# A hybrid attention, convolution and ConvFFN block: up tiles of one side of two groups, sums in three batches, another opening

## The chip, the cores and the metric

The kernel runs on one core of a Trainium2 chip. The time is the device time of one execution in microseconds (us). A profiled execution gives the trace; its rows name the engines PE (matmul), PEld (PE's weight loads), DVE, ACT, POOL and SP. In this kernel SP issues nearly all transfers and POOL a few.

## The reference

One sequence of 256 tokens, width 2048, all float32. A conditioning vector c gives six vectors of 2048 (shift, scale and gate for each half of the block), and each half is a gated residual:

```python
mod = jax.nn.silu(c) @ w_ada[l] + b_ada[l]                # 2048 x 12288
sh1, sc1, g1, sh2, sc2, g2 = jnp.split(mod, 6, axis=-1)
h = modulate(rms_norm(x, norm1_g[l]), sh1, sc1)           # h * (1 + scale) + shift
proj = h @ w_in[l]                                        # 2048 x 6144
q, k, v, gb, gc, xt = jnp.split(proj, ...)                # 8 heads of 128 | 1024 conv channels
attn = moba_attention(q, k, v)                            # 256 tokens: one block, plain causal
conv = gb * causal_dwconv(gc * xt, conv_w[l], conv_b[l])
mixed = concat([rms_norm(attn, ...), rms_norm(conv, ...)])
x = x + g1 * (mixed @ w_out[l])                           # 2048 x 2048
h2 = modulate(rms_norm(x, norm2_g[l]), sh2, sc2)
u = causal_dwconv(h2 @ w_ffn_up[l], ffn_conv_w[l], ffn_conv_b[l])   # 2048 x 11264, 3 taps
u_gate, u_up = jnp.split(u, 2, axis=-1)
x = x + g2 * ((jax.nn.silu(u_gate) * u_up) @ w_ffn_down[l])         # 5632 x 2048
```

## The kernel before

Every float32 factor is split into a rounded part `hi` and a rest `lo`, and a product is made of three: hi·hi and hi·lo of the activations with `hi` of the weights, and hi of the activations with `lo` of the weights. A weight tile is 1 MB (128 x 4 x 512): SP loads it into one of seven `raw` buffers, ACT rounds it to `hi` (`split_hi`, L329), DVE subtracts to `lo` (`split_lo`, recorded at L166, the line of the helper through which most of DVE's work goes), and PE multiplies. There are three `hi` and three `lo` buffers. The work on one weight tile is a slot, and the slots follow one another on PE in a fixed order.

Opening. SP loads x, then four tiles of `w_ada` (L363) for the first 256 channels of the scale SC1 and the shift SH1, then weights of the projection. PE multiplies the four tiles with silu(c) (`ada`, L396) into partial sums on 128 rows; ACT copies them (`adae`), PE transposes the copy (`adac`, L453), DVE reduces it (`adaz`), and ACT adds it to the normed, scaled input `hf`, which gives the first `h`. Then the first projection product can run (L583). The other modulation tiles are spread over later slots by the table `ada`; each is consumed by PE or by DVE (L387, L389).

Projections. 48 tiles of `w_in` in the order of `turns` (L514 to L517), with attention and convolution between, to about 324 us; then `w_out`, to about 424 us.

Up. A group is 256 channels of each side (gate and up). Its slot k takes four of the 16 row blocks of `w_up`, 256 columns of the gate side and 256 of the up side, in two transfers of 512 KB (`up_slots`). The sixteen 512-wide products are L1057, the sixteen 256-wide ones L1060; they add up in four PSUM banks `z`. Groups 0 to 5 are done in two halves of the rows ('a' and 'b'; L1042 for the first four in 'a'). Groups 6 to 21 ('x') run from 570 us on. `up_sum` adds the halves of a bank on ACT and DVE (`ub`), `up_conv` and `up_conv_b` make the three-tap convolution (`uy`): a first tap on ACT, each further one on ACT (`tap`) with a sum on DVE, or as two STTs on DVE (scalar times tensor plus tensor). `up_silu` and `up_gate` make the product.

Down. The product with `w_down` of groups 0 to 15 is done by Strassen's scheme: seven products in place of eight. A group's `w_down` tile is used in two half slots, 'A' (three products' worth) and 'B' (four, from sums of blocks that DVE makes at L301, L304, L307), for each half `cp` of the columns (L994 to L998). Half slots stand between up slots; `places` in `plan` lists for every group behind which of its slots 0 to 3 they stand. At the end of a batch the bank sums `u` are copied (`pu`, ACT) and POOL adds them to DRAM (`down_sums`). `join_load` reads these back and `join_sum` joins them on DVE (`ju`). The last six groups go through twelve ordinary down slots (keys `('D', f)`), and `evac_down` writes the output. In these, `gate_down` multiplies with G2, whose modulation tiles are spread over the up slots.

What a slot's steps on ACT, DVE, SP and POOL are queued behind is set by tables: a step is hung to a slot (`at`), and the classes `cls` order the steps within a slot; `x_first` and `hi_late` set where `lo` and `hi` stand among them.

Of the kernel before, what the change touches and what calls it, by code (L numbers as in the profile page):

```python
# [59 lines left out]
       'taps': [1, 1, 2, 6],  # L60
# [10 lines left out]
       'slag': [[1, 2], [-1, 2]],  # L71
# [5 lines left out]
       'up': [[0, 2, 2, 4], [0, 0, 0, 0]],  # L77
       'gate': [3, 4, 7, 11],
# [6 lines left out]
               'conv_q': 0,  # L85
# [36 lines left out]
               'join_sum': 2},  # L122
       'up0': [[1, 1, 2, 4], [0, 1, 3, 3], [0, 2, 1, 2], [1, 1, 3, 5], [4, 4, 5, 8], [5, 5, 6, 9]],
# [16 lines left out]
       'part_lead': [4, 3, 2],  # L140
# [7 lines left out]
def tile_block(  # L148
# [77 lines left out]
    V.tensor_copy(identb, ident)  # L226

# [118 lines left out]
    class Ada:  # L346


        def __init__(self, part, c0, n, pe):
            self.part, self.c0, self.n, self.pe = part, c0, n, pe  # L350
            self.rows = 2048 // n
            self.tiles = NK // self.rows
            self.nch = n // P
            self.acc = None
            self.two = []
            self.used = 0

        def want(self, r):
            a = self.part * D + self.c0 * P
            k0 = r * self.rows  # L360

            def issue(t):
                nc.sync.dma_start(self.view(t), w_ada[0, k0 * P:(k0 + self.rows) * P, a:a + self.n]  # L363
                                  .rearrange("(k p) f -> p k f", p=P))
            return issue

# [172 lines left out]
    def pair_load(k, f):  # L539
        def issue(t):  # L540

            n = 1 if not slots_begun else 2
            slots_begun.append(f)
            for j in range(0, 2, n):
                nc.sync.dma_start(t.rearrange("p (k h) f -> p k (h f)", k=2)[:, j:j + n],
                                  w_in[0, (k + j) * P:(k + j + n) * P, COL[f] * 512:COL[f] * 512 + 1024]
                                  .rearrange("(k p) f -> p k f", p=P))
# [274 lines left out]
    def up_sum(grp, one):  # L822

        new = grp not in ub
        if one:
            if new:
                ub[grp] = [t2k(f"ub{grp}") for _ in range(2)]
            for ft in range(4):
                p, d = zp[grp][ft][:, :256], ub[grp][ft // 2][:, (ft % 2) * 256:(ft % 2) * 256 + 256]
# [4 lines left out]
            del zp[grp]  # L834
            return
        c = [t2k(f"ub{grp}") for _ in range(2)]
        for ft in range(4):
            act(c[ft // 2][:, (ft % 2) * 256:(ft % 2) * 256 + 256], zp[grp][ft][:, 256:], AF.Copy)  # L838
# [814 lines left out]
```

## Time and profile before

| | us |
|---|---|
| median of three runs | 1146.89 (1146.16 to 1148.3) |
| the profiled execution's own time | 1144.87 |
| its span, first to last instruction | 1143.1 |
| PE busy | 1128.9 (99%) |
| DVE busy | 1064.0 (93%) |
| ACT busy | 730.6 (64%) |
| moved by DMA | 363.66 MB, mean 318 GB/s |

A row of the timeline gives start, duration, engine, line, instruction, names and shapes, and in brackets the idle time ahead and who ended it. Runs of like instructions stand in one row with their number. The DMA share is the mean busy share of the core's 16 DMA engines.

### The profile page before, as it was taken

The page shows a single profiled execution, that of the slowest core. Times are in us where ns is not written, and L with a number is a line of the kernel's source. Part 1 is how long each engine was busy: PE and PEld are TensorE (multiplying, and loading weights), DVE is VectorE, ACT ScalarE, POOL GpSimd, SP SyncE. Part 2 cuts the span into 40 slices and gives each one's busy share as a digit, 9 for nine tenths or more (in the row PEclk, how much of TensorE's full clock was granted, in tenths as well). Part 3 has the DMA queues.
Part 4 walks back from the last instruction along what each step waited for, and adds up shares of the span by engine and source line. Part 5 has one row for each costly group of instructions (what it writes and reads, how often), then busy time and mean ns, then how long its engine had stood idle before and what let it go on. Part 6 is the DMA issues. An engine that isn't in the chain of part 4 may idle for free.

```text
span 1143.1 us, 16244 instructions
## 1 busy us (share of the span) xinstructions
PE 1128.9 (99%) x6035; PEld 953.8 (83%) x6035; DVE 1064.0 (93%) x1163; ACT 730.6 (64%) x1090; POOL 61.3 (5%) x90
## 2 busy tenths in 40 slices
PE   6999999999999999999999999999999999999998
PEld 4777778888888889988888888888888888888887
DVE  4789989989999998889999999899999999999798
ACT  4644455576786555566687676777677768866731
POOL 1000000000000000000000000101011101111000
PEclk9999999999999999999999999999999999999999
DMA  9999998998898899987679887999899988999951
GB/s 362 407 413 399 412 370 300 415 381 306 331 395 315 288 317 356 330 278 243 215 244 370 308 292 245 315 361 297 312 275 339 318 315 265 350 318 298 366 224 74
DMA packets 198687, 363.66 MB, mean 318 GB/s; under 512 B 9408, under 2 KB 108180, under 8 KB 194000
## 3 DMA queue, kind: packets, MB, share of 16 engines
q1 hardware_dynamic: 189152, 343.44, 82.8%
q0 software_dynamic: 8160, 17.04, 6.8%
q10 hardware_dynamic: 1296, 2.16, 0.5%
q8 instruction: 47, 0.77, 0.2%
q14 instruction: 32, 0.26, 0.1%
HBM read 343.70 MB, written 18.89 MB: 317 GB/s over the span
## 4 chain that ended last, share of the span: by engine, by line
PE 93%; DVE 3%; DMA 2%; SPq 1%; ACT 1%; issue 0%; DVEq 0%; ACTq 0%
PE z L1057 25%; PE z L1060 13%; PE u L996 4%; PE u L998 4%; PE u L994 4%; PE z L1042 4%; DMA raw<-in_w_in_dram 2%; DVE lo L166 2%; PE mk L516 1%; PE mk L517 1%; PE mk L514 1%; PE mx L516 1%; PE mc L516 1%; PE mq L517 1%; PE mg L516 1%; PE mx L517 1%
## 5 line engine op out<-in xcount | busy, mean ns | idle before, releaser
L329 ACT ACTIVATE hi<-raw 128x2048 fp32r<-128x2048 f32 (+1 forms) x227 | 417.8, 1857 | 260.5 <-DMA raw<-in_w_in_dram 73.2
L166 DVE TENSOR_TENSOR lo<-raw,hi 128x2048 fp32r<-128x2048 f32 (+2 forms) x229 | 501.7, 2200 | 23.0 <-ACT hi L329 17.7
L1057 PE MATMUL z<-h,hi 128*128 128x512 f32 x1280 | 303.3, 390 | 0.2 <-DVE ub L166 0.2
L1057 PEld LDWEIGHTS z<-h,hi 128*128 128x128 f32 x1280 | 237.8, 188 | 49.5 <-ACT hi L329 0.8
L389 DVE SCALAR_TENSOR_TENSOR ada<-raw,csil,ada 128x512 f32<-128x512 f32 (+3 forms) x167 | 195.7, 1175 | 5.3 <-DMA raw<-in_w_ada_dram 1.8
L1060 PEld LDWEIGHTS z<-h,lo 128*128 128x128 f32 x1280 | 163.1, 191 | 5.6
L1060 PE MATMUL z<-h,lo 128*128 128x256 f32 x1280 | 165.0, 283 | 0.0
L996 PE MATMUL u<-hi,gh 128*128 128x512 f32 x224 | 88.1, 393 | 0.0
L998 PE MATMUL u<-hi,gl 128*128 128x512 f32 x224 | 87.7, 392 | 0.0
L994 PE MATMUL u<-lo,gh 128*128 128x512 f32 x224 | 61.4, 390 | 0.0
L806 ACT ACTIVATE uy<-ub,fc,fc 128x256 f32<-128x256 f32 x88 | 47.6, 596 | 12.8 <-DVE ub L166 12.7
L938 POOL DMA_DIRECT2D down_sums<-pu x42 | 36.6, 1287 | 304.1 <-ACT pu L934 304.1
L996 PEld LDWEIGHTS u<-hi,gh 128*128 128x128 f32 x224 | 42.2, 188 | 9.9 <-ACT pu L934 2.8
L994 PEld LDWEIGHTS u<-lo,gh 128*128 128x128 f32 x224 | 42.0, 188 | 9.1 <-DVE lo L166 0.3
L998 PEld LDWEIGHTS u<-hi,gl 128*128 128x128 f32 x224 | 42.2, 189 | 7.4
L817 ACT ACTIVATE tap<-ub,fc 128x256 f32<-128x256 f32 x96 | 41.7, 502 | 0.0
L166 DVE TENSOR_TENSOR ub<-z,ub 128x256 f32<-128x256 f32 x96 | 33.8, 413 | 6.8 <-ACT ub L838 6.8
L301 DVE TENSOR_TENSOR raw<-raw 128x1024 f32<-128x1024 f32 x32 | 39.0, 1218 | 0.9 <-DMA raw<-in_w_ffn_down_dram 0.9
L1042 PE MATMUL z<-h,hi 128*128 128x256 f32 x256 | 36.4, 284 | 0.2 <-ACT h L765 0.2
L838 ACT ACTIVATE ub<-z 128x256 f32<-128x256 f32 x96 | 28.6, 383 | 12.1 <-PE z L1057 12.1
L166 DVE TENSOR_TENSOR uy<-tap,uy 128x510 f32<-128x510 f32 (+1 forms) x48 | 32.8, 684 | 2.0 <-ACT tap L817 0.2
L166 DVE SCALAR_TENSOR_TENSOR uy<-ub,fc,uy 128x254 f32<-128x254 f32 (+1 forms) x80 | 33.6, 477 | 0.6
(460 smaller groups left out, 1764.7 us busy)
## 6 DMA issues: line engine op xcount, KB each, us to landing
raw<-in_w_ada_dram SPq DMA_DIRECT2D x96, 1024.0 KB, 7.5
raw<-in_w_ffn_up_dram SPq DMA_DIRECT2D x176, 512.0 KB, 6.1
raw<-in_w_in_dram SPq DMA_DIRECT2D x47, 1024.0 KB, 8.0
raw<-in_w_ffn_down_dram SPq DMA_DIRECT2D x44, 1024.0 KB, 9.3
raw<-in_w_out_dram SPq DMA_DIRECT2D x16, 1024.0 KB, 6.0
raw<-in_w_ffn_down_dram SPq DMA_DIRECT2D x32, 512.0 KB, 5.0
down_sums<-pu POOLq DMA_DIRECT2D x56, 256.0 KB, 8.3
raw<-in_w_ffn_down_dram SPq DMA_DIRECT2D x32, 256.0 KB, 5.4
```

The lines of the kernel that those rows point to most:

```text
L166: f(*a, **k)
L329: act(hi[:, :n], t[:, :n], AF.Copy)
L389: W.scalar_tensor_tensor(out=self.acc, in0=t[:, j, :], scalar=csil[:, i:i + 1], in1=self.acc, op0=ALU.mult, op1=ALU.add)
L516: mm(o, a, hi[:, k, s], start=(first and k == 0), stop=False)
L806: act(y[:, s], b[:, s], AF.Identity, bias=bias[:, i + j:i + j + 1], scale=w[2][:, i + j:i + j + 1])
L817: act(z[:, s], b[:, s], AF.Copy, scale=w[2 - d][:, i + j:i + j + 1])
L994: mm(bank_of(key), a, lo[:, n], start=False, stop=j in ends)
L996: mm(bank_of(key), a, hi[:, n], start=key not in begun, stop=False)
L998: mm(bank_of(key), b, hi[:, n], start=False, stop=False)
L1042: mm(o, w[:, j, a], h2T[k + j][:, v * 256:v * 256 + 256], start=begins and j == 0 and w is hi and not v, stop=ends and j == 3 and v == 1)
L1057: mm(zp[grp][ft], hi[:, j, ft * P:(ft + 1) * P], h2T[k + j], start=begins and j == 0, stop=ends and j == 3 and not late)
L1060: mm(zp[grp][ft][:, :256], lo[:, j, ft * P:(ft + 1) * P], h2T[k + j][:, :256], start=False, stop=ends and j == 3 and late)
```

## The change

Four things change together.

1. An up tile holds 512 columns of one side, the 256 of group g and the 256 of group g + 1, in one transfer of 1 MB with runs of 2 KB instead of two with runs of 1 KB. Group numbers of slots now alternate between the gate side and the up side of a pair; `up_sum` and `up_conv` work on a side of two groups, and gating follows behind the up side.
2. Strassen's sums are stored in three batches of 6, 5 and 5 groups instead of four of 4, with another distribution of half slots, all of which now stand in `places`. 42 transfers to `down_sums` remain of 56. The taps table turns 32 STTs of the convolution on DVE into 32 products on ACT and 16 sums on DVE.
3. The opening: 34 products of constants (`one`, `two`, 128x128) stand between the steps on PE; the fourth modulation tile is loaded and multiplied in two halves; the reduction of its sums is two products with a 0/1 vector instead of transposes and a DVE reduction; the first weight tile comes in four pieces, rounded by ACT and DVE in turn; `h` of the first channels is formed on DVE.
4. Const tiles are allocated in another order (`ssq` earlier). In both programs all the wide tiles start at multiples of 512 bytes.

With it come new values of the ordering tables. Three lines of those, and the code:

```diff
-                 [[0, 1, 2, 3], [4, 5, 6, 7], [8, 9, 10, 11], [12, 13, 14, 15]], ...
+                 [[0, 1, 2, 3, 4, 5], [6, 7, 8, 9, 10], [11, 12, 13, 14, 15]], ...
-               [1, 2, 256, True, 1, 2], ...
+               [1, 2, 256, True, 1, 1], ...
-       'taps': [1, 1, 2, 6],
+       'taps': [1, 2, 2, 6],
...
+        def products(self, r, i, j):
...
+            for k in range(i, j):
+                q = 32 * (k % 4)
+                mm(self.acc[q:q + 32, :], crep[:, self.rows * r + k, :], self.held[:, k, :], ...)
+            if j == self.rows:
+                load_next()
...
-            for a, b in zip(ub[grp], c):
-                V.tensor_tensor(out=a, in0=a, in1=b, op=ALU.add)
...
+        for i in range(2):
+            if new:
+                ub[g + i, w] = c[i]
+            else:
+                V.tensor_tensor(out=ub[g + i, w], in0=ub[g + i, w], in1=c[i], op=ALU.add)
...
-            slots.append((w_load(w_up, k, 4, [(grp * 256, 256), (DFF + grp * 256, 256)]), 4, go))
+            slots.append((w_load(w_up, k, 4, [(grp % 2 * DFF + grp // 2 * 512, 512)]), 4, go))
...
+    ada_init[1].cuts[1] = [(0, 4), (4, 8)]
...
+    def keep_busy(b, n):
+        for _ in range(n):
+            mm(b[:, 256:384], onesr, onesr, start=True, stop=True)
...
+    w0, w1, w2, w3, w4, w5 = CFG["busy"]
+    keep_busy(p_one, w0)
...
+    sh.products(1, 0, 4)
+    sh.products(1, 4, 8)
+    keep_busy(p_one, w4)
+    rows_sum = t2k("adae")[:, :256]
+    act(rows_sum, sh.acc, AF.Copy)
+    for k in range(2):
+        mm(p_one[:, k:k + 1], rows_sum[:, k * P:(k + 1) * P], sel, start=k == 0, stop=k == 1)
+    keep_busy(bank("two"), w5)
+    z = small(8, "adaz")[:, :2]
+    V.tensor_copy(z, p_one[:, :2])
...
+    act(hi[:, 0], w[:, 0], AF.Copy)
+    for k in range(2):
+        hT[k] = halves(hk[k])
+        if k:
+            act(hT[k][0], hf[k], AF.Identity, bias=z[:, k:k + 1])
+        else:
+            V.tensor_scalar(hT[k][0], hf[k], z[:, k:k + 1], None, op0=ALU.add)
```

PE at the end of the opening, before, from the third modulation tile (`ada`, of SH1) to the first projection product (`mc`); `xn` are transposes of x:

```order
L396 MATMUL ada0_0_219<-raw_108,crep_89 32x256 x8
L1489 MATMUL xn6_230<-ident_69,xr_100 128x128 x2
L1489 MATMUL xn7_233<-ident_69,xr_100 128x128 x2
L1489 MATMUL xn6_230<-ident_69,xr_102 128x128 x2
L1489 MATMUL xn7_233<-ident_69,xr_102 128x128 x2
L396 MATMUL ada0_0_219<-raw_110,crep_89 32x256 x8
L453 MATMUL adac0_0_268<-ident_69,adae0_0_256 128x128 x2
L583 MATMUL mc00_293<-hi_258,h0_261 128x512
```

The same stretch after:

```order
L383 MATMUL ada0_0_246<-raw_109,crep_91 32x256 x8
L1515 MATMUL xn6_257<-ident_69,xr_101 128x128 x2
L1515 MATMUL xn7_260<-ident_69,xr_101 128x128 x2
L1515 MATMUL xn6_257<-ident_69,xr_103 128x128 x2
L1515 MATMUL xn7_260<-ident_69,xr_103 128x128 x2
L1528 MATMUL one_180<-onesr_76 128x128 x5
L383 MATMUL ada0_0_246<-raw_111,crep_91 32x256 x8
L1528 MATMUL one_180<-onesr_76 128x128 x5
L1573 MATMUL one_180<-ssq_87,adae_289 128x1 x2
L1528 MATMUL two_293<-onesr_76 128x128 x6
L608 MATMUL mc00_334<-hi_302,h0_304 128x512
```

Sixteen constant products stand in three gaps here (eighteen more ahead of this stretch), and two 1-wide products stand where the transposes of `adae` were. The last modulation tile is one row in both, but its transfer comes in two halves.

SP, before, from the first weight tile on (`128x8x256` are modulation tiles of 256 columns):

```order
L545 DMA raw_112<-in_w_in_dram 128x1024 x2
L545 DMA raw_115<-in_w_in_dram 128x2x1024
L545 DMA raw_174<-in_w_in_dram 128x2x1024
L363 DMA raw_201<-in_w_ada_dram 128x8x256
L363 DMA raw_228<-in_w_ada_dram 128x8x256
L545 DMA raw_254<-in_w_in_dram 128x2x1024
L363 DMA raw_279<-in_w_ada_dram 128x8x256
L363 DMA raw_285<-in_w_ada_dram 128x8x256
L545 DMA raw_291<-in_w_in_dram 128x2x1024
```

And after:

```order
L568 DMA raw_114<-in_w_in_dram 128x512 x4
L570 DMA raw_119<-in_w_in_dram 128x2x1024
L570 DMA raw_178<-in_w_in_dram 128x2x1024
L371 DMA raw_209<-in_w_ada_dram 128x8x256
L371 DMA raw_255<-in_w_ada_dram 128x8x256
L371 DMA raw_282<-in_w_ada_dram 128x8x256
L570 DMA raw_320<-in_w_in_dram 128x2x1024
L371 DMA raw_326<-in_w_ada_dram 128x8x256
L570 DMA raw_332<-in_w_in_dram 128x2x1024
```

`raw_228` and `raw_285` before, `raw_255` and `raw_282` after, are the two tiles that PE consumes for the next channels of SC1; the second has moved ahead of a weight tile, and on PE it now directly follows the first. From the last row on, the order of kinds and sizes is the same in both programs up to the modulation tile that PE uses at 62.37 us.

ACT at the end, before, behind the copies (`ub`) of the last up group's banks:

```order
L881 ACTIVATE gh_9973<-uy_9057 128x512
L881 ACTIVATE gh_9975<-uy_9390 128x512
L806 ACTIVATE uy_9981<-ub_9959,fc_1744,fc_1740 128x256 x2
L817 ACTIVATE tap<-ub_9959,fc_1736 128x256 x2
L806 ACTIVATE uy_9990<-ub_9960,fc_1744,fc_1740 128x256 x2
L817 ACTIVATE tap<-ub_9960,fc_1736 128x256 x2
L817 ACTIVATE tap<-ub_9960,fc_1732 128x256 x2
L863 ACTIVATE uy_9981<-uy_9981 128x512
L329 ACTIVATE hi<-raw 128x2048 x3
```

And after:

```order
L831 ACTIVATE uy_9845<-ub_9831,fc_1785,fc_1781 128x256 x2
L842 ACTIVATE tap<-ub_9831,fc_1777 128x256 x2
L842 ACTIVATE tap<-ub_9831,fc_1773 128x256 x2
L831 ACTIVATE uy_9856<-ub_9832,fc_1785,fc_1781 128x256 x2
L842 ACTIVATE tap<-ub_9832,fc_1777 128x256 x2
L842 ACTIVATE tap<-ub_9832,fc_1773 128x256 x2
L959 ACTIVATE pu<-u_9554 128x512
L959 ACTIVATE pu<-u_9557 128x512
L959 ACTIVATE pu<-u_9560 128x512
L959 ACTIVATE pu<-u_9563 128x512
L453 ACTIVATE adar_9919<-adab_9914 128x512
L335 ACTIVATE hi<-raw 128x2048 x2
```

The `pu` copies of the last batch (before a whole group earlier) now stand here, between the convolution and the third and fourth `hi` of the down tiles; the `gh` have moved behind.

More of the change, by code (lines that the diff above doesn't have):

```diff
@@ L226, in tile_block @@
     V.tensor_copy(identb, ident)
+    ssq = const.tile([P, 32], F32, name="ssq")
+    sel = ssq[:, :1]
+    V.tensor_reduce(out=sel, in_=ident.rearrange("p (j r) -> p j r", j=4)[:, :, 0], axis=AX.X, op=ALU.add)
     rows(vb, [(by_p(norm1_g[0]), 16)], nc.gpsimd)
@@ L356, in __init__ @@
             self.used = 0
+            self.cuts = {}
         def want(self, r):
@@ L362, in issue @@
             def issue(t):
-                nc.sync.dma_start(self.view(t), w_ada[0, k0 * P:(k0 + self.rows) * P, a:a + self.n]
-                                  .rearrange("(k p) f -> p k f", p=P))
-            return issue
+                for i, j in self.cuts.get(r, [(0, self.rows)]):
+                    nc.sync.dma_start(self.view(t)[:, i:j], w_ada[0, (k0 + i) * P:(k0 + j) * P, a:a + self.n]
+                                      .rearrange("(k p) f -> p k f", p=P))
+            return issue
+        def products(self, r, i, j):
+            if i == 0:
+                self.used += 1
+                self.held = self.view(take((self, r)))
+            if self.acc is None:
+                self.acc = bank(f"ada{self.part}_{self.c0}")[:, :self.n]
+            for k in range(i, j):
+                q = 32 * (k % 4)
+                mm(self.acc[q:q + 32, :], crep[:, self.rows * r + k, :], self.held[:, k, :],
+                   start=r == 0 and k < 4, stop=r == self.tiles - 1 and k >= self.rows - 4,
+                   tile_position=(0, q))
+            if j == self.rows:
+                load_next()
         def home(self):
@@ L540, in issue @@
         def issue(t):
[L542 to L547, printed above, removed]
+            if not slots_begun:
+                slots_begun.append(f)
+                for j in range(4):
+                    a = (COL[f] + j % 2) * 512
+                    nc.sync.dma_start(t[:, j], w_in[0, (k + j // 2) * P:(k + j // 2 + 1) * P, a:a + 512])
+                return
+            nc.sync.dma_start(t.rearrange("p (k h) f -> p k (h f)", k=2),
+                              w_in[0, k * P:(k + 2) * P, COL[f] * 512:COL[f] * 512 + 1024]
+                              .rearrange("(k p) f -> p k f", p=P))
         return issue
@@ L820, in tile_block, with up_sum @@
     ub, uy = {}, {}
-    def up_sum(grp, one):
-        new = grp not in ub
+    def up_sum(u, one):
+        g, w = u // 2 * 2, u % 2
+        new = (g, w) not in ub
         if one:
             if new:
-                ub[grp] = [t2k(f"ub{grp}") for _ in range(2)]
+                ub.update({(g + i, w): t2k(f"ub{g + i}") for i in range(2)})
             for ft in range(4):
-                p, d = zp[grp][ft][:, :256], ub[grp][ft // 2][:, (ft % 2) * 256:(ft % 2) * 256 + 256]
+                p, d = zp[u][ft][:, :256], ub[g + ft // 2, w][:, (ft % 2) * 256:(ft % 2) * 256 + 256]
                 if new:
@@ L1511, in xn_norm @@
                             in1=rT.unsqueeze(1).to_broadcast([P, 2, 256]), op=ALU.mult)
-    xn_norm(0, 1, 2, 3)
-    ada_init[0].consume(1)
-    ada_init[0].evac()
-    ada_init[0].cols()
-    xn_norm(4)
+    sc, sh = ada_init
+    n0, n1, n2 = CFG["norm_at"]
+    xn_norm(*range(n0))
+    sc.consume(1)
+    keep_busy(p_one, w1)
+    sc.evac()
+    sc.cols()
+    hf = []
+    b1 = SH1 * NK
+    for k in range(2):
+        hf.append(t1k("hf"))
+        V.tensor_scalar(hf[k], xnT[0][:, k * 256:(k + 1) * 256], A1[:, k:k + 1], bcol[:, b1 + k:b1 + k + 1],
+                        op0=ALU.mult, op1=ALU.add)
@@ L1550, in tile_block @@
+    rest(0)
+    V.tensor_copy(hi[:, 1], w[:, 1])
+    rest(1)
+    act(hi[:, 2], w[:, 2], AF.Copy)
+    V.tensor_copy(hi[:, 3], w[:, 3])
+    xn_norm(*range(n1, n2))
+    for j in range(0, 4, 2):
+        V.tensor_tensor(out=lo[:, j:j + 2], in0=w[:, j:j + 2], in1=hi[:, j:j + 2].bitcast(F32), op=ALU.subtract)
+    xn_norm(*range(n2, 8))
     splits.append((hi, lo))
```

136 lines of the change are left out of this document (62 added, 74 removed), and 18 rows, old and new, of the table CFG.

## The prediction

> **What bounds the kernel now.** I read the line of busy time first, then each engine's busy time by stage. The stages begin at 0; at 22.4, the first product of a projection; at 62.4; at 425, the first up products; at 473; at 570, the up groups with half slots; at 1073.7, the last down products; and at 1139.8, when the products end.
>
> ```profile
> PE 1128.9 (99%) x6035; PEld 953.8 (83%) x6035; DVE 1064.0 (93%) x1163; ACT 730.6 (64%) x1090; POOL 61.3 (5%) x90
> ```
>
> The rows by stage have the window and its length, busy time and count of PE, PEld, DVE, ACT and POOL, then PE's granted clock, the DMA share and GB/s.
>
> ```profile
> 0.00:22.40 22.40, 12.74 (x106) 8.48 (x106) 9.47 (x28) 10.15 (x15) 5.24 (x16) 1.00 0.96 349
> 22.40:62.40 40.00, 39.29 (x192) 29.14 (x193) 31.39 (x40) 25.18 (x33) 0.00 (x0) 0.96 1.05 407
> 62.40:425.00 362.60, 362.60 (x1778) 293.71 (x1778) 340.42 (x366) 215.61 (x412) 7.13 (x11) 1.00 0.94 357
> 425.00:473.00 48.00, 47.76 (x400) 47.52 (x398) 42.95 (x52) 24.77 (x35) 2.31 (x2) 1.00 1.03 364
> 473.00:570.00 97.00, 97.00 (x560) 85.82 (x559) 91.47 (x131) 63.43 (x105) 0.00 (x0) 1.00 0.75 251
> 570.00:1073.70 503.70, 503.46 (x2688) 433.31 (x2687) 484.00 (x479) 365.97 (x465) 46.11 (x60) 1.00 0.94 308
> 1073.70:1139.80 66.10, 66.05 (x326) 55.79 (x324) 63.92 (x72) 25.46 (x29) 0.56 (x1) 1.00 0.51 196
> ```
>
> From 62.4 to 1139.8 PE lacks 0.24 + 0.24 + 0.05 = 0.53 us of 1077.4. A busy PE need not be a fast one, so the next look is at its pace, in the chain of waits:
>
> ```profile
> 492.16 7.28 PE z L1057 x32
> 499.44 3.83 PE z L1060 x32
> 784.17 3.94 PE z L1057 x16
> ```
>
> Thirty-two 512-wide products take 7.28 us, 227 ns each; thirty-two 256-wide ones 3.83, 120 ns. Per sixteen that is 3.64 and 1.92, and an up slot costs 5.56. The third row is the one group of sixteen in the chain that is slow, by 3.94 − 3.64 = 0.3 us. So time can come only from the opening, where PE idles 22.40 − 12.74 = 9.7 us; from that 0.3; and from products that disappear. None do: both programs have the same projection, up and down products.
>
> **The opening: its own chain.** The timeline's rows to the first product, and the granted clock behind it:
>
> ```profile
> 19.61 1.07 PE L396 MATMUL ada<-raw,crep 128*32 128x256 f32 x16 [0.54 <-DMA raw<-in_w_ada_dram]
> 20.74 0.38 ACT L417 ACTIVATE adae<-ada 128x256 f32<-128x256 f32 x1 [5.01 <-PE ada L396]
> 21.18 0.44 PE L453 MATMUL adac<-ident,adae 128*128 128x128 f32 x2 [0.50 <-ACT adae L417]
> 21.66 0.17 DVE L166 TENSOR_REDUCE adaz<-adac 128x2 f32<-128x8 f32 x1
> 21.86 0.51 ACT L1542 ACTIVATE h<-hf,adaz 128x256 fp32r<-128x256 f32 x1 [0.73 <-DVE adaz L166]
> 22.42 5.43 PE L583 MATMUL mc<-hi,h 128*128 128x512 f32 x16 [0.80 <-ACT h L1542]
> ```
>
> ```profile
> 22.40:25.40 3.00, 2.98 (x7) 2.40 (x8) 0.77 (x2) 1.46 (x2) 0.00 (x0) 0.50 1.03 425
> ```
>
> The fourth modulation tile lands at 19.6 and 2.8 us of small steps follow. The change cuts that tile in two, so half of its 1.07 us of products goes ahead of the last landing (−0.5). Two 1-wide products take the place of two transposes; bounded by nothing and by the transposes' 0.44, they save 0 to 0.4, and I take 0.3, since their width is nearer to nothing. DVE's forming of h stands against ACT's 0.51: nothing. First product at 21.6, a gain of 0.8.
>
> Then seven products run in 3 us at half clock, 427 ns each: 7 × 0.2 = 1.4 us lost, 1.6 with the products that straddle the ends. The 34 constant products fill waits ahead of that. One costs at most the 0.22 of a transpose and at least a quarter of 0.227, so 1.9 to 7.5 us for all, inside 9.7 of idle time. Eleven stand behind the fourth tile, 0.6 to 2.4 us, beside the copy, z and h that take 0.38 + 0.17 + 0.51 anyway: 0, with +1.3 as the upper end. What they do to the clock no row of this trace shows; the ends are 0 and −1.6.
>
> The Trainium skill's page "TensorE: Matmul & The Clock Gate" (Part 1: The HAM clock gate) says that PE drops to half clock after an idle window of some 3.4 us and comes back after a busy one. The row at 0.50 behind 9.7 us of idle PE agrees. By that rule the constant products earn the whole 1.6, and rival A below is its time.
>
> I take −1.6, since 0.50 was granted while PE was 2.98 of 3.00 busy: what came before it decides. Slot 0 then gains 2.4 us. Whether that reaches the end is another question.
>
> **The opening: its cover.** At a share of 1.05 from 22.4 to 62.4, a tile lands when the bytes ahead of it are through, whoever computes how early.
>
> ```profile
> 35.03 1.07 PE L396 MATMUL ada<-raw,crep 128*32 128x256 f32 x16
> 36.48 1.92 ACT L329 ACTIVATE hi<-raw 128x2048 fp32r<-128x2048 f32 x1 [4.00 <-DMA raw<-in_w_in_dram]
> 41.88 1.07 PE L396 MATMUL ada<-raw,crep 128*32 128x256 f32 x16
> 46.82 0.50 PE L516 MATMUL mx<-hi,h 128*128 128x512 f32 x1 [0.47 <-ACT pa_g L531]
> 56.91 0.50 PE L517 MATMUL mq<-hi,hl 128*128 128x512 f32 x1 [0.16 <-DVE hl L166]
> 57.00 1.92 ACT L329 ACTIVATE hi<-raw 128x2048 fp32r<-128x2048 f32 x1 [0.86 <-DMA raw<-in_w_in_dram]
> 59.60 1.92 ACT L329 ACTIVATE hi<-raw 128x2048 fp32r<-128x2048 f32 x1 [0.68 <-DMA raw<-in_w_in_dram]
> 62.37 1.06 PE L396 MATMUL ada<-raw,crep 128*32 128x512 f32 x8
> 64.70 3.11 DVE L389 SCALAR_TENSOR_TENSOR ada<-raw,csil,ada 128x512 f32<-128x512 f32 x4 [0.41 <-DMA raw<-in_w_ada_dram]
> 67.11 1.92 ACT L329 ACTIVATE hi<-raw 128x2048 fp32r<-128x2048 f32 x1 [0.67 <-DMA raw<-in_w_in_dram]
> ```
>
> Four landings were waited for: 57.0, 59.6, 64.7, 67.1. In SP's order one more tile stands between the second and the third. The others are about 2.5 apart, so it lands at (59.6 + 64.7)/2 = 62.1. PE uses it at 62.37: 0.3 us of slack. The changed program has the same tiles, of the same sizes, ahead of it on SP, and the same 144 projection products ahead of its use on PE. However early the opening ends, PE stands there until 62.1.
>
> An earlier wall takes most already. The second group of SC1's modulation products (41.88) moves from behind slot 2 to directly behind the first group (35.03), and its tile takes the place in SP's order of the one that landed at 36.5. PE waits there for 36.5, does the group by 37.5 and slot 2, 36.03 to 41.88 less what waiting was in it, some 5.5, by 43.0; before, slot 2 and that group ended at 42.88. From there to 62.37 are 19.5 us with two waits of 0.47 and 0.16; without them PE is at the tile at 43.0 + 18.9 = 61.9, still ahead of it. With them it comes at 62.5. The opening is worth between +0.1 and −0.3; I take −0.3, as the code moved around both waits. PE has no gap from 62.4 to 425, so that is kept.
>
> **The up tiles.** The 176 transfers of 512 KB become 88 of 1 MB, with runs of 2 KB instead of 1.
>
> ```profile
> raw<-in_w_ffn_up_dram SPq DMA_DIRECT2D x176, 512.0 KB, 6.1
> 434.42 2.29 DVE L166 TENSOR_TENSOR lo<-raw,hi 128x2048 fp32r<-128x2048 f32 x1 [2.29 <-DMA raw<-in_w_ada_dram]
> ```
>
> The stretch from 425 is the place where that could count: the stream is full there (1.03), at 364 GB/s against 407 with the projections' longer runs. Half-length runs might cost up to 48 × (1 − 364/407) = 5 us of transfer. But DVE waits for tiles there (second row) while PE lacks 0.24 us: the buffered tiles cover the rest, and the 5 us are worth 0 to −0.24. I take 0. SP's 88 fewer issues and what queues behind them have the same cover. The tiles' addresses add and remove no instruction and no byte, and PE at its pace could not pay for them: 0 as well.
>
> **Three batches of sums** instead of four: POOL's transfers go from 56 to 42, beside PE. ACT loses 14 pu copies and gains 32 taps; DVE loses 32 of the STTs and gains 16 sums of taps.
>
> ```profile
> L817 ACT ACTIVATE tap<-ub,fc 128x256 f32<-128x256 f32 x96 | 41.7, 502 | 0.0
> L166 DVE TENSOR_TENSOR uy<-tap,uy 128x510 f32<-128x510 f32 (+1 forms) x48 | 32.8, 684 | 2.0 <-ACT tap L817 0.2
> L166 DVE SCALAR_TENSOR_TENSOR uy<-ub,fc,uy 128x254 f32<-128x254 f32 (+1 forms) x80 | 33.6, 477 | 0.6
> L166 DVE TENSOR_TENSOR lo<-raw,hi 128x2048 fp32r<-128x2048 f32 (+2 forms) x229 | 501.7, 2200 | 23.0 <-ACT hi L329 17.7
> L301 DVE TENSOR_TENSOR raw<-raw 128x1024 f32<-128x1024 f32 x32 | 39.0, 1218 | 0.9 <-DMA raw<-in_w_ffn_down_dram 0.9
> ```
>
> DVE: −32 × 0.477 + 16 × 0.684 = −4.3 us of its 484.0 in 503.7; ACT: 32 × 0.5 − 14 × 0.5 = +9 of 366, with 138 free. PE lacks 0.24 there, so none of it can pay. What can is the 0.3 at 784.17: a group that ends without a half slot in its last place, so the next one comes onto PSUM banks that DVE is still emptying. The new table has such places only where the banks are free: −0.3.
>
> **The end.** In the new table the last half slot stands directly ahead of the down products (at D), where before a whole group, 4 × 5.56 = 22 us, lay between. Behind the last up products, at D − 2.7 (a half slot is 12 × 0.227), stand on ACT the copy, both convolutions, then the four pu copies and only then hi of the third down tile; on DVE four sums of taps, two products, the joining sums and lo of the third tile.
>
> ```profile
> 1073.85 1.18 ACT L838 ACTIVATE ub<-z 128x256 f32<-128x256 f32 x4
> 1075.94 1.10 ACT L806 ACTIVATE uy<-ub,fc,fc 128x256 f32<-128x256 f32 x2
> 1078.71 1.71 ACT L817 ACTIVATE tap<-ub,fc 128x256 f32<-128x256 f32 x4
> 1085.27 4.54 DVE L166 TENSOR_TENSOR ju<-ju 128x512 f32<-128x512 f32 x7
> down_sums<-pu POOLq DMA_DIRECT2D x56, 256.0 KB, 8.3
> ```
>
> ACT ends its taps at D − 2.7 + 1.2 + 2 × (1.1 + 1.7) = D + 4.1. DVE ends the sums of taps at D + 4.8, two 128x512 products (0.7 each) at 6.2, the joining sums at 10.7, lo at 12.9. PE needs it at D + 2 × 5.45 + 16 × 0.227 = 14.5. ACT's hi (1.9) follows the four pu copies, 0.5 each like the taps, and lands near D + 8 against 10.9. The second join loads what POOL's transfers add up (8.3 us behind pu, D + 6 to 9: about D + 17); behind it on SP wait the last four down tiles, first needed at D + 8 × 5.45 = 43. So 0, with 1.6 us to spare.
>
> **Sum.** −0.3 − 0 − 0.3 + 0 = −0.6 us. The profiled execution took 1144.87 (span 1143.1 and 1.77 around it), 2.0 under the median of 1146.89; I carry the difference over: 1144.3 there, 1146.3 as a median.
>
> **Rivals.**
> A. The opening pays in full. If the stream of tiles isn't rigid, since a faster PE frees buffers earlier and the queues run further ahead, slot 0's 2.4, the two waits (0.6) and the 0.3 at 784 come through: 1146.9 − 3.3 = 1143.6. For it: that PE waits are named by releasers on ACT and DVE too. Against: the share of 1.05, and 2.5 us between landings in any order of use. Chance 0.14.
> B. Slower, through DVE in the last up groups. The new table puts eight second-half slots (B) into the last two groups. Each costs DVE a lo of 2.2 and sums of 1.2 + 2 × 0.7, 4.8 us, against PE's 2.7. For the two groups DVE has 16 × 2.2 + 7 × 2.6 + 2 × 1.4 (ub) + 8 × 0.7 (taps) + 7 × 0.65 = 66.3 us, PE 8 × 5.56 + 8 × 2.72 = 66.2. No air is left, and the joining sums then stand ahead of the third down tile. It decides when DVE comes to the last up products more than 1.6 us late. Each further us is one of PE; two or three groups with DVE at 96% on average can make a debt of 5, so +3.4: 1150.3. Against: the stage's DVE has 4.3 us less to do in all. Chance 0.25.
> C. Nothing comes of it: the waits at 46.8 and 56.9 stay under other names and 784's moves elsewhere. 1146.9, chance 0.15.
>
> **How the numbers follow.** My forecast has 0.46. A measurement here tells a change of 0.2%, 2.3 us, from none; the runs shown spread over 2.1. The forecast and C lie within it (0.61), A beyond it below (0.14), B above (0.25). The range takes A's time with its run spread, 1143.0, and B's, 1150.5. Either can go beyond its own time about as often as not, which leaves 2 in 10 outside.
>
> **What would show it.** The first product near 21.6 and PE's granted clock over 0.9 behind it show the opening's chain; a PE wait of about 2 us for the second SC1 tile near 36, and the ada products of 62.37 at 62.1, show the wall. An opening stage that reaches these products below 61 makes A right. Up slots at 5.56 with a smaller DMA share in 425 to 473 show that the runs paid in DMA only. No slow group of sixteen near 784 shows the −0.3. PE lacking more than 1 us between 570 and 1139.8, with "DVE lo" as the releaser, most of all at the third down tile, shows B. A prediction off by over 3 us without one of these would mean that PE's own pace moved.

## The result and the profile after

| | before | changed |
|---|---|---|
| median of six runs, us | 1146.47 (1144.93 to 1148.3) | 1156.3 (1154.44 to 1159.2) |
| ratio to before | | 1.0088 (95%: 1.0076 to 1.0100) |
| span of the profiled execution | 1143.1 | 1153.1 |

Forecast was 1146.3, in a range of 1143.0 to 1150.5. The changed kernel is 0.9% slower, outside the range, where a gain of 0.6 us was forecast.

The stages of the changed kernel, cut at the times that the prediction used (the last down products start at 1077.1 now, not at 1073.7; the columns are those of the prediction's table of stages):

```profile
0.00:22.40 22.40, 16.07 (x140) 12.40 (x141) 7.78 (x26) 10.22 (x16) 5.25 (x16) 1.00 0.95 350
22.40:62.40 40.00, 37.54 (x190) 27.90 (x190) 32.58 (x44) 24.70 (x33) 0.00 (x0) 1.00 1.05 406
62.40:425.00 362.60, 362.46 (x1773) 293.33 (x1771) 341.31 (x366) 215.44 (x412) 8.35 (x12) 1.00 0.94 356
425.00:473.00 48.00, 46.64 (x388) 46.43 (x389) 43.63 (x53) 24.14 (x32) 1.39 (x2) 1.00 0.91 339
...
570.00:1073.70 503.70, 502.29 (x2679) 433.39 (x2678) 481.97 (x467) 368.04 (x478) 28.44 (x38) 1.00 0.87 298
1073.70:1149.80 76.10, 71.53 (x343) 58.89 (x341) 66.85 (x73) 29.33 (x35) 6.00 (x9) 0.98 0.57 193
```

PE lacks 1.4 us from 425 to 473 (0.24 before), 1.4 in the half-slot stage (0.24) and 4.6 from 1073.7 on (0.05). Of the 4.6, 1.9 lie behind the last product, at 1147.9, since the last window ends after it; 2.65 are a single wait. Following the same products through both traces shows where the 10.0 us of span went:

| from, to | before, us | changed, us | more |
|---|---|---|---|
| start to the modulation products of 62.37 | 62.37 | 63.08 | 0.7 |
| to the first up product | 363.55 | 364.84 | 1.3 |
| to the first of the last down products | 647.82 | 649.16 | 1.3 |
| to the end of the products | 66.01 | 70.80 | 4.8 |
| to the end of the span | 3.32 | 5.18 | 1.9 |

The largest share is at the end. DVE's timeline in the changed kernel has one long idle stretch there, and PE's a wait behind it:

```profile
1103.81 0.69 DVE L169 TENSOR_TENSOR ju<-ju,ada 128x512 f32<-128x512 f32 x1 [7.64 <-DMA ada<-gate_sums]
1114.48 1.92 PE L536 MATMUL m('D', 0)0_9931<-lo,gh 128*128 128x512 f32 x4 [2.65 <-DVE lo L169]
```

`ada<-gate_sums` is the broadcast of G2, which gates the sums of the down stage. POOL's timeline shows how it came late, first in the kernel before, then in the changed one:

```profile
1069.08 1.97 POOL L433 DMA_DIRECT2D gate_sums<-adar  x4 [12.97 <-ACT adar L431]
1076.36 0.56 POOL L439 DMA_DIRECT2D ada<-gate_sums  x1 [5.31 <-DMA gate_sums<-adar]
```

```profile
1080.45 3.49 POOL L963 DMA_DIRECT2D down_sums<-pu  x4 [41.15 <-ACT pu L959]
1082.62 3.27 POOL L455 DMA_DIRECT2D gate_sums<-adar  x4
1094.48 0.56 POOL L461 DMA_DIRECT2D ada<-gate_sums  x1 [8.59 <-DVE lo L169]
```

The issue of the broadcast names DVE's `lo` as what ended its wait, but the last of the four `gate_sums` lands at 1093.86, and the issue follows 0.6 us behind it, as it does before (0.7 us behind a landing at 1075.69). The broadcast itself lands at 1103.8, just where DVE goes on.

The row `slag` of the tables, which the prediction did not price, moves G2's sums from one slot ahead of the last down products to their start, and the broadcast by one slot. There the sums' copy on ACT stands behind the four `pu` copies of the half slot that now ends the stage, and their transfers on POOL behind four `down_sums`. The broadcast is issued 18 us later than before; 3.3 of these come from the down products, which themselves start later. The product `ju<-ju,ada` and all later steps of DVE wait for it, the seven sums `ju<-ju` and `lo` of the seventh down tile among them.

### The profile page after: what moved, and what is told of

The parts are those of the page before. It is cut to its first block, busy times and chain, and to the rows that moved or that the text cites. A ratio compares the mean times of both kernels' runs of the same rounds, so it can differ in the third digit from the quotient of the medians.

```text
span 1153.1 us, 16070 instructions
## 1 busy us (share of the span) xinstructions
PE 1133.5 (98%) x6071; PEld 958.5 (83%) x6071; DVE 1063.9 (92%) x1150; ACT 735.2 (64%) x1108; POOL 49.4 (4%) x76
## 3 DMA queue, kind: packets, MB, share of 16 engines
q10 hardware_dynamic: 1296, 2.16, 0.5%
## 4 chain that ended last, share of the span: by engine, by line
PE 80%; DVE 14%; DMA 4%; issue 2%; ACT 1%; SPq 0%; DVEq 0%; ACTq 0%
PE z L1082 24%; PE z L1085 12%; DVE lo L169 6%; PE u L1019 4%; PE u L1023 4%; PE u L1021 4%; PE z L1067 4%; DVE ada L411 2%; PE mk L538 1%; PE mk L539 1%; PE mk L536 1%; PE mx L538 1%; PE mq L539 1%; PE mc L538 1%; PE mv L538 1%
## 5 line engine op out<-in xcount | busy, mean ns | idle before, releaser
L1082 PEld LDWEIGHTS z<-h,hi 128*128 128x128 f32 x1280 | 238.2, 188 | 50.6 <-DVE ub L169 2.1
L842 ACT ACTIVATE tap<-ub,fc 128x256 f32<-128x256 f32 x128 | 54.5, 506 | 0.0
L169 DVE TENSOR_TENSOR uy<-tap,uy 128x510 f32<-128x510 f32 x64 | 43.9, 685 | 3.5
L963 POOL DMA_DIRECT2D down_sums<-pu x28 | 24.4, 1287 | 283.0 <-ACT pu L959 283.0
L1067 PEld LDWEIGHTS z<-h,hi 128*128 128x128 f32 x256 | 33.1, 192 | 0.5 <-ACT h L790 0.5
```

Source lines behind the costliest of these rows:

```text
L169: f(*a, **k)
L842: act(z[:, s], b[:, s], AF.Copy, scale=w[2 - d][:, i + j:i + j + 1])
L1067: mm(o, w[:, j, a], h2T[k + j][:, v * 256:v * 256 + 256], start=begins and j == 0 and w is hi and not v, stop=ends and j == 3 and v == 1)
L1082: mm(zp[grp][ft], hi[:, j, ft * P:(ft + 1) * P], h2T[k + j], start=begins and j == 0, stop=ends and j == 3 and not late)
```

## The experiments

Twelve kernels, each an edit of the changed one (`a_`) or of the one before (`b_`). Ratios are to the kernel before on the same chip, with 95% intervals.

**Where the end lost its time.** Two edits, each of one number:

```diff
a_slag:  -'slag': [[2, 2], [0, 3]]           +'slag': [[2, 2], [-1, 2]]
a_half:  -[0, 1, 2, 3, 3], [0, 2, 3]         +[0, 1, 2, 3, 3], [0, 2, 2]
```

> The changed kernel with the G2 sums one slot and their broadcast one slot earlier (as in the kernel before). Theory Q (the 7.64 us that DVE waits for the G2 broadcast at 1103.81 come from the queue: the G2 sums' copy stands behind the four pu copies on ACT and their transfers behind down_sums on POOL): the sums' transfers now go ahead of the last down_sums and land within 6 us of issue instead of 9; the broadcast still stands behind down_sums, so it lands at the end of those plus 3 to 7 us. DVE's wait falls from 7.6 to 0 to 4 us, the down stage from 70.8 to 66 to 69, and the time from 1156.3 to 1150 to 1154. The sums need a PSUM bank just when all eight are taken, which may cost PE up to 1.5 us there. Rival L (the last half slot right ahead of the down products overloads ACT and DVE, whatever the order of the small transfers): DVE loses the same time under other names, and the time stays within 1 us of 1156.3.

> The changed kernel with its last half slot one up slot earlier (5.6 us), nothing else. Theory Q: the pu copies and down_sums leave before the G2 sums, which then land within about 6 us; the broadcast is there about 1096, DVE waits 0 to 1 us instead of 7.6, the down stage takes 66 to 67 us instead of 70.8, the tail 3.3 instead of 5.2: 1149.5 to 1151. Rival S (only the slots given to sums and broadcast count, not what stands ahead of them on ACT and POOL): those are unchanged here, so 1155.5 to 1157.

a_slag: 1151.09, ratio 1.0053 (1.0034 to 1.0072). a_half: 1150.09, 1.0037 (1.0024 to 1.0050). Both are within what the theory of the late transfers gave, and neither rival survives: a_half leaves the slots of sums and broadcast as they are, and a_slag leaves the last half slot where it is. In a_slag the sums land 4.5 to 5.0 us behind their issue, and the broadcast, at 1098.20, just as DVE comes to it; the price on PE that was expected is there too, a wait of 0.82 at 1074.9 for a bank. Down stage and tail take 65.98 and 3.58 us. In a_half the broadcast lands at 1095.4 and DVE, at it by 1097.8, doesn't wait. Its down stage and tail:

```profile
1078.60:1144.80 66.20, 66.15 (x328) 55.95 (x324) 63.60 (x71) 25.16 (x27) 2.53 (x5) 1.00 0.58 207
1144.80:1148.30 3.50, 0.00 (x0) 0.00 (x0) 0.41 (x1) 0.00 (x0) 0.00 (x0) 0.86 0.32 109
```

66.2 and 3.5 us, about as before. So it takes both changes of the tables, the later half slot and the later sums, to lose the 6 at the end: with either taken back, the down stage is at 66 again.

**Norm2.** In the changed kernel DVE's two products `n2d` take 1.85 us instead of 0.48 while POOL clears the accumulator of G2, whose first tile the tables bring seven up slots earlier. First the changed kernel, then a_memset, where that tile stands five slots later:

```profile
424.09 1.80 POOL L393 MEMSET ada<- 128x2048 f32 x1 [89.03 <-PE ada L418]
424.19 1.85 DVE L169 TENSOR_SCALAR n2d<-ident,n2r 128x128 f32<-128x128 f32 x2
426.12 0.68 PE L763 MATMUL n2b<-n2d,ones 128*128 128x128 f32 x4 [1.26 <-DVE n2d L169]
```

```profile
424.44 0.48 DVE L169 TENSOR_SCALAR n2d<-ident,n2r 128x128 f32<-128x128 f32 x2
425.04 0.71 PE L763 MATMUL n2b<-n2d,ones 128*128 128x128 f32 x4
```

```diff
a_memset:  -'gate_rows': [3, 10,     +'gate_rows': [8, 10,
b_memset:  -'gate_rows': [10, 14,    +'gate_rows': [3, 14,
```

> The changed kernel with the first G2 tile five up slots later, so that the accumulator's memset on POOL no longer falls on norm2. Theory M (the two n2d products on DVE took 1.85 us instead of 0.48 because POOL's memset of 128x2048 ran at the same time, 424.09 to 425.89): n2d takes 0.48 again, PE's wait ahead of n2b goes from 1.26 to under 0.1, and from 62.4 to the first up product 1.3 us are gained: 1155.0. Rival (another cause on DVE there): n2d keeps 1.85 and the time stays at 1156.3.

> The kernel before with the first G2 tile seven up slots earlier, where the changed kernel has it. Theory M: the memset falls on norm2, n2d takes 1.5 to 2 us instead of 0.48, PE waits 1 to 1.4 us ahead of n2b: 1147.7, 1.2 us over before. Rival: no change there, 1146.5.

b_memset, the kernel before with the memset put on norm2:

```profile
423.40 1.80 POOL L371 MEMSET ada<- 128x2048 f32 x1 [95.48 <-DMA raw<-in_w_ada_dram]
423.56 1.79 DVE L166 TENSOR_SCALAR n2d<-ident,n2r 128x128 f32<-128x128 f32 x2
425.43 0.68 PE L738 MATMUL n2b<-n2d,ones 128*128 128x128 f32 x4 [1.26 <-DVE n2d L166]
```

The mechanism is shown from both sides, 1.26 us of PE each time. The times are not what was expected: b_memset 1148.79, 1.0024 (1.0014 to 1.0035), 2.9 over before rather than 1.2, and a_memset 1157.08, 1.0098 (1.0083 to 1.0114), no gain. Moving the tile also moves DVE's work on it (2.3 us a tile): a_memset has new PE waits at 491 and 505 (0.51 and 0.43), and one of 1.90 at 659 where the changed kernel has 1.16; b_memset has three from 751 to 757 (1.13, 0.78 and 0.31). That these waits come from the moved work is likely by the place, and not separated further.

**The opening.** a_quiet leaves out the 34 constant products, a_p1 puts the second SC1 tile back.

```diff
a_quiet:  -'busy': [9, 4, 5, 5, 5, 6]        +'busy': [0, 0, 0, 0, 0, 0]
a_p1:     -[1, 2, 256, True, 1, 1]           +[1, 2, 256, True, 1, 2]
```

> The changed kernel without its 34 constant products. Theory W (what the opening gains is taken by the wait for the second SC1 tile, which lands near 36.5 whatever PE does before): the first slot is slow again, PE's granted clock near 0.5 for some 3 us behind the first product, the first slot 1.5 us longer, the wait at 36.5 shorter by as much; the fourth tile group of modulation products at 63 stays within 0.3 us, and the time at 1156.3 within 0.7. Rival (the constant products pay to the end): 1.6 us slower, 1157.9. Rival (they stand in the way of the first product): the first product comes 0.3 to 0.5 us earlier than 22.4 to 22.8.

> The changed kernel with the second SC1 tile and its products one slot later again, as in the kernel before. Theory W: PE no longer waits 1.5 us near 36.5; it then meets the tile that lands at 62.1, so the modulation products there move from 63.08 to 62.1 to 62.5, 0.6 to 1.0 us: 1155.5. Rival R (the stream of tiles is not rigid): they move to 61.0 to 61.5, 1154.5.

a_quiet: 1155.15, 1.0087 (1.0072 to 1.0102), which overlaps the changed kernel's interval. The first product comes at 21.94 against 22.85, and the clock is full all the same, with no constant product in the program:

```profile
22.40:25.40 3.00, 3.00 (x15) 2.52 (x14) 2.94 (x5) 0.07 (x1) 0.00 (x0) 1.00 1.02 420
```

So the part of the expectation that rested on the clock failed: the half clock of the one profile of before was not this opening's rule. b_memset, with the opening of before, has full clock there as well. The constant products bought nothing here, and the first product came 0.9 us later with them (22.38 to 22.85 in nine of the profiles that have them).

In the other two profiles that have them, a_spread and a_three (both below), the first product came at 25.33 and 25.48. PE's products ran there at half pace up to about 18 us, though the granted clock reads 1.00; nine of the constant products, first in the changed kernel, then in a_spread:

```profile
12.87 1.22 PE L1528 MATMUL one<-onesr 128*128 128x128 f32 x9
```

```profile
13.05 2.18 PE L1528 MATMUL one<-onesr 128*128 128x128 f32 x9
```

PE has no idle time there, so its own queue, constants included, set the start. Why it ran slowly is open. These two kernels also show best that the start does not reach the end: the modulation products of the second wall stand at 63.1 in a_spread, as in the changed kernel, and at 62.9 in a_three, since the waits on the way (1.35 and 0.47) are gone there.

```profile
25.33 0.93 PE L608 MATMUL mc<-hi,h 128*128 128x512 f32 x3
63.11 1.07 PE L418 MATMUL ada<-raw,crep 128*32 128x512 f32 x8
```

a_p1: 1153.87, 1.0068 (1.0051 to 1.0085). The wait near 36.5 is gone, and these products stand at 61.86, 1.2 us earlier, of which 0.7 are left at the first up product. This lies between the two expectations, 62.1 to 62.5 and 61.0 to 61.5. The tile landed at 61.7 there, and in other profiles between 61.55 (a_quiet) and 62.06 (before, where 62.1 was worked out), so the stream gave way by no more than landings differ from one execution to the next. The time is below what either theory gave, but its interval overlaps the changed kernel's.

**The up tiles' runs.** The same tiles by two transfers each:

```diff
a_runs1k:  -w_load(w_up, k, 4, [(grp % 2 * DFF + grp // 2 * 512, 512)])
           +w_load(w_up, k, 4, [(grp % 2 * DFF + grp // 2 * 512 + h, 256) for h in (0, 256)])
```

> The changed kernel with each up tile loaded by two transfers of 256 columns, runs of 1 KB instead of 2, nothing else moved. If the runs pay in DMA time only: the DMA share in 425 to 473 goes from 0.91 back to about 1.0, PE loses at most 0.5 us there; between 640 and 660, where the stream is full (1.04), the first tile of a B half lands later and PE's wait at 657.84 grows by 0 to 1.5 us: 1156.3 to 1158.3. If the longer runs carry the schedule: 3 us or more slower, 1159.5.

1159.07, 1.0116 (1.0101 to 1.0131): some 2.8 us over the changed kernel, between the two expectations, the intervals just apart. The stretch from 425 to 473 shows nothing of it: PE 46.94, and a share of 0.94, where about 1.0 was expected. So the runs are worth only 0.03 of the share there; its fall from 1.03 to 0.91 comes mostly from fewer bytes (364 GB/s before, 339 in the changed kernel, 338 in a_runs1k), since modulation tiles have moved out of this stretch. b_memset, the kernel before with one such tile moved and its short runs kept, has 0.94 and 338 too.

The waits that grew are in the half-slot stage, 2.14 at 658.5 and 1.80 at 852.3. Waits of both sizes also occur there in kernels with long runs (a_p1 3.04 at 659, a_hilate 1.96 at 658.3 and 1.72 at 852), so which of them the runs cause is open. By the times the long runs are likely worth something in this schedule, and not the 0 of the prediction; no trace shows where.

**The wait at 658.** In the changed kernel the group behind ten half slots waits for its banks. Rows of DVE, ACT and PE:

```profile
652.29 1.23 DVE L307 TENSOR_TENSOR raw<-raw 128x1024 f32<-128x1024 f32 x1 [2.30 <-DMA raw<-in_w_ffn_down_dram]
655.14 1.92 ACT L335 ACTIVATE hi<-raw 128x2048 fp32r<-128x2048 f32 x1 [4.29 <-PE u L1023]
656.97 1.18 ACT L864 ACTIVATE ub<-z 128x256 f32<-128x256 f32 x4
657.84 3.01 PE L1082 MATMUL z<-h,hi 128*128 128x512 f32 x12 [1.16 <-DVE ub L169]
```

The first B tile lands at 652.3; its block sums, its `hi` and behind that the copies `ub` follow. Three edits:

```diff
a_spread:  -[[], [0, 1], [0, 0, 0, 1, 2, 2, 2, 2, 2, 3],   +[[3], [0, 1, 2, 3], [0, 0, 1, 2, 2, 2, 3],
a_hilate:  -'hi_late': [..., 80, 82]                       +'hi_late': [..., 80, 82, 111]
a_three:   -[0, 0, 0, 1, 2, 2, 2, 2, 2, 3],                +[0, 0, 0, 1, 2, 2, 2, 3, 3, 3],
```

> The changed kernel with three of the ten half slots of group 8 moved to groups 6 and 7. Theory D (ten half slots of 2.04 us, each with 0.75 MB, fill the DMA stream from 640 on, so the first B tile lands late, DVE's block sums at 652.29 wait for it, ACT's hi for these, and the copy of the up banks behind that hi): the DMA share in 640 to 660 falls under 1, PE's wait at 657.84 (1.16) goes to under 0.3, and the time to 1154.7 to 1155.3. Rival (the order on ACT and DVE alone makes the wait): it stays at 1.2 to 1.9 and the time at 1156.3.

> The changed kernel with one step moved on ACT: behind the last up slot of group 8 the copies of its banks (ub) go ahead of the rounding (hi) of the first B tile instead of behind it. Theory O (the PE wait of 1.2 to 3.2 us near 658 is ACT's order: ub stands behind a hi that waits for DVE's block sums, and these for a late tile): ub starts near 654 instead of 657, the wait falls under 0.3, and the time by 1.0 to 2.0 us, to 1154.3 to 1155.3. Rival (the late tile itself stops PE): the wait only moves to the product that needs the tile, one slot later, and the time stays within 0.5 of 1156.3.

> The changed kernel with two of the five half slots that stand in a row behind slot 2 of group 8 moved behind its slot 3; no other slot changes place. Theory D2 (five half slots in a row use tiles every 2.04 us, faster than the stream brings them, so the tiles behind them queue for up to 13 us and the first B tile lands at 652 instead of 648): with at most three in a row the share in 640 to 660 falls, PE's wait near 658 goes from 1.2 to 2.3 us to under 0.5, and the time from 1156.3 by 1 to 2 us to 1154.3 to 1155.3. Rival (the ten half slots of the group are too many however they stand): the wait keeps 1 us or more, 1156 or over.

a_spread: 1160.41, 1.0127 (1.0112 to 1.0143), a miss. The wait at 658 is gone, but the `cp` halves now change over without an up slot between, and PE waits for the banks that `pu` has yet to copy:

```profile
628.84 0.50 PE L1021 MATMUL u<-hi,gh 128*128 128x512 f32 x1 [1.48 <-ACT pu L959]
631.98 0.50 PE L1021 MATMUL u<-hi,gh 128*128 128x512 f32 x1 [2.41 <-ACT pu L959]
```

a_hilate: 1157.22, 1.0095 (1.0074 to 1.0116), no gain. `ub` starts at 651.91 on ACT now, and the wait stays:

```profile
651.91 1.82 ACT L864 ACTIVATE ub<-z 128x256 f32<-128x256 f32 x4 [1.37 <-PE z L1085]
652.98 1.23 DVE L307 TENSOR_TENSOR raw<-raw 128x1024 f32<-128x1024 f32 x1 [2.94 <-DMA raw<-in_w_ffn_down_dram]
657.77 1.41 DVE L169 TENSOR_TENSOR ub<-z,ub 128x256 f32<-128x256 f32 x4
658.25 3.01 PE L1082 MATMUL z<-h,hi 128*128 128x512 f32 x12 [1.96 <-DVE ub L169]
```

DVE's half of the sums stands behind the block sums too, and these behind the tile. So it isn't ACT's order but DVE's, with the late tile ahead of both.

a_three: 1155.83, 1.0078 (1.0056 to 1.0099). PE is busy 20.00 of 20.00 us between 640 and 660, and the wait is gone. But the DMA share stayed at 1.04 and the first B tile lands at 651.4 instead of 652.3, against what was expected of a burst that fills the stream. What changed is DVE's order and the cover: the group's last up slot ends 4 us earlier (649.3), three half slots rather than one stand behind it, and DVE's half of the sums runs ahead of the block sums:

```profile
649.38 1.42 DVE L169 TENSOR_TENSOR ub<-z,ub 128x256 f32<-128x256 f32 x4 [1.52 <-ACT ub L864]
652.38 1.22 DVE L307 TENSOR_TENSOR raw<-raw 128x1024 f32<-128x1024 f32 x1
```

So DVE's order behind the last up slot makes the wait, as a_hilate had it. Order and cover moved together in a_three, and no run separates them. The gain in time is not resolved: the interval overlaps the changed kernel's, the stage from the first up product to the down products is no shorter (651.3 us against 649.2), and waits of 1.37 at 850 and 0.59 at 860 stand in it.

**All together.** a_all has the edits of a_half, a_p1 and a_hilate, and `gate_rows` from 5; a_all2 has those of a_half, a_p1 and a_three, and `gate_rows` from 5.

> The changed kernel with four edits together: the last half slot one up slot earlier, the second SC1 tile back behind slot 2, ub ahead of hi behind group 8, and the first G2 tile two up slots later (so that the memset leaves norm2). If the causes found add up: -6.2, -0.6, -1.5 and -1.0 from 1156.3 give 1147.0, with a range of 1145.5 to 1148.5, which is the time before within 0.2%. If they hide one another, or DVE in the half-slot stage is the bound behind them: 1149 to 1151.

> The kernel of a_all without the step moved on ACT and with the two half slots moved as in a_three. By theory D2 the 3.6 us that PE still lost between 640 and 660 there fall to 1 or less: from 1148.45 to 1146.0 to 1147.0, the time before within 0.15%. By its rival: 1148 to 1149. Faster than before by more than 0.2% is expected by neither.

a_all: 1148.45, 1.0023 (1.0012 to 1.0034), with a PE wait of 2.16 still at 656.7 and half clock for 3.4 us behind it. a_all2: 1147.4, 1.0006 (0.9995 to 1.0017), no measurable difference from before; it was expected at 1146.0 to 1147.0, with 1148 to 1149 for the rival, and lies between. PE is busy 20.00 of 20.00 us from 640 to 660. The stages of its profile:

```profile
425.00:473.00 48.00, 47.76 (x400) 47.52 (x398) 44.01 (x52) 24.09 (x33) 2.30 (x2) 1.00 0.96 352
570.00:1076.80 506.80, 505.33 (x2692) 434.72 (x2692) 483.59 (x468) 372.42 (x485) 31.92 (x42) 1.00 0.88 298
1076.80:1143.00 66.20, 65.60 (x323) 55.42 (x321) 63.44 (x69) 24.62 (x26) 2.52 (x5) 1.00 0.58 207
```

Five numbers of the tables account for its loss. With them mended, long runs, three batches and the new opening together are worth nothing that can be measured.

## Why the prediction failed

- The step that failed is "The end ... So 0, with 1.6 us to spare". The term measured +6.7 (4.8 in the down stage, 1.9 in the tail). The path it walked was right as far as it went: `lo` of the third down tile ended 11.2 us behind the first down product where 12.9 was estimated, with 14.5 allowed. It left out another step in the same queues: G2's sums and broadcast, which the tables had moved. The prediction followed the second join behind `pu` and `down_sums`; POOL's order in the changed program has `gate_sums` behind them as well. The runs showed in its place that DVE stands idle for 7.64 us for the broadcast and PE for 2.65 us behind DVE, with half clock for 3.4 us after that; a_slag and a_half each bring the stage back to 66 us.
- Rival B had the sign, the place and the engine (DVE at the end), and the wrong mechanism: DVE was not overloaded but idle for 7.64 us, in line for a transfer. Its chance of 0.25 was for a debt of DVE's work, which shows at most in small waits: 0.18 at 862.9 in the changed kernel, 0.3 to 0.65 near 860 in its edits.
- "The opening is worth between +0.1 and −0.3" measured +0.7. PE's timeline in the changed kernel has the first wall and what followed it:

```profile
22.85 3.89 PE L608 MATMUL mc<-hi,h 128*128 128x512 f32 x16
36.55 1.07 PE L418 MATMUL ada<-raw,crep 128*32 128x256 f32 x16 [1.35 <-DMA raw<-in_w_ada_dram]
41.53 0.50 PE L538 MATMUL mv<-hi,h 128*128 128x512 f32 x1 [0.47 <-ACT pa_g L553]
56.91 0.50 PE L538 MATMUL mq<-hi,h 128*128 128x512 f32 x1 [0.41 <-ACT h L1203]
57.63 0.50 PE L539 MATMUL mq<-hi,hl 128*128 128x512 f32 x1 [0.22 <-DVE hl L169]
```

  The wall at 36.5 stood as worked out. The relief of the waits behind it (0.47 and 0.16 before) did not come: they are 0.47, 0.41 and 0.22 now, as rival C had it. So PE reaches the products of the second wall at 63.1, behind the tile and not waiting for it. The gain ahead of the first wall was mis-sized as well: the first product was forecast 0.8 earlier and came 0.4 later. The constant products, priced at nothing with +1.3 as the upper end, are the likely price of it, since without them it came at 21.94: 0.4 to 0.9 us in nine profiles, 3.4 and 3.5 in two. But a_quiet's second wall at 62.7 shows how little of that passes the first.
- The −1.6 for the clock was read from one execution. Granted clock 1.00 stands there in every other profile, with constants or without. Nor do the 9.7 us of idle PE lie in one piece: 5.8 of them are before 9 us, the later waits are under 1 us each, and the clock reads 1.00 up to 22.2. The Trainium skill's page "TensorE: Matmul & The Clock Gate" (Part 1: The HAM clock gate) says that the window over which idleness is judged runs free and does not begin with the kernel. An opening that falls to half clock in one profile and not in another agrees with that, but no run here separates it.
- Norm2 was priced at 0 by silence: the prediction did not ask what POOL does there. It measured 1.26 us of PE.
- The −0.3 at 784 came (no slow group there), and the same kind of wait came back larger at 658 with 1.16, behind DVE's order with one half slot to cover it. At 748 some 0.4 came back; there PE waits in part for `hi`, and the cause is not shown. "784's moves elsewhere" in rival C came true.
- The up tiles' 0 held where it was argued, in 425 to 473: PE gained nothing there. The smaller share, named as a sign that the runs paid in DMA, does not show it, since a_runs1k with short runs has 0.94 against 0.91. For the half-slot stage the 0 was likely too simple, by the times of a_runs1k.

## What to carry to other kernels

Where a change comes with a table of positions, price every moved step that issues a transfer, the small ones too: 8 KB of sums, moved one slot on and queued behind 1 MB of accumulation, cost some 6 us here, when the whole change was forecast at −0.6. Look at what else stands in the queue of the transfer that a late engine waits for, and let the sum begin at the engine that is idle, not at the one that is busy. And a gain at the start of a kernel is worth what is left of it at the next landing that the start doesn't hurry.

## What the runs showed of the hardware

A transfer on POOL's queue landed behind the larger ones ahead of it: the four `gate_sums` took 5.1 to 5.2 us from issue to landing before, and 9.8 to 10.6 in the changed kernel, where they landed 0.2 to 0.9 us behind the last `down_sums`. In a_slag, with none ahead, they took 4.5 to 5.0; in a_half 6.2 to 7.1, 0.2 to 0.7 behind the last `down_sums`.

Two 128x128 DVE products stood still for as long as POOL's memset ran: together they took 1.75 to 1.87 us instead of 0.48, in every profile where the two met.

PE's clock fell to half behind single waits of 1.8 to 3.0 us, but not behind each of them. The windows of the changed kernel show PE idle, and then 0.54 for 3.4 us:

```profile
1111.80:1114.40 2.60, 0.04 (x1) 0.00 (x0) 2.60 (x3) 0.00 (x0) 0.00 (x0) 1.00 0.09 35
1114.40:1117.80 3.40, 3.32 (x8) 2.63 (x9) 3.40 (x3) 0.00 (x0) 0.00 (x0) 0.54 0.00 0
1117.80:1121.20 3.40, 3.40 (x15) 2.74 (x15) 3.40 (x3) 1.92 (x1) 0.00 (x0) 0.96 0.00 0
```

The next two windows stand behind a wait of 1.79 in a_runs1k and behind one of 2.39 in a_quiet:

```profile
1117.70:1121.10 3.40, 3.40 (x9) 2.61 (x9) 3.40 (x2) 0.00 (x0) 0.00 (x0) 0.50 0.00 0
```

```profile
1114.50:1117.90 3.40, 3.39 (x15) 2.78 (x16) 3.40 (x2) 0.00 (x0) 0.00 (x0) 1.00 0.00 0
```

Waits of 1.86 and 2.41 (a_spread), 2.16 (a_all), 2.46 (a_three) and 3.04 (a_p1) were followed by half clock too; waits of 1.90 (a_memset), 1.96 (a_hilate) and 2.14 (a_runs1k, at 658.5) were not. So the length of the wait alone does not decide it. Half clock for 3.4 us is 1.7 us of PE's pace, but not all of it was lost here: in a_quiet, at full clock, the down products take 70.5 us against 70.8, as PE waits for DVE again at 1131.4, for 1.39.

The Trainium skill's page "TensorE: Matmul & The Clock Gate" (Part 1: The HAM clock gate) has PE at half clock after at least one idle window of about 3.4 us. Every wait listed here was shorter than that, so on this point the measurement decides.
